# Mixture of experts: 32 slots as the stationary operand in plain float32, four column tiles of the array, weights used as they come from memory

## The chip, the cores and the metric

The kernel runs on one core of one Trainium2 chip. The metric is the device time of one launch, in microseconds (us). A core has a matrix engine (PE, with its weight loads shown apart as PEld), a vector engine (DVE), a scalar engine (ACT), a general engine (POOL) and a queue engine (SP) that here issues almost all loads; 16 DMA engines carry them out. Products are accumulated in PSUM, in banks; everything else lies in SBUF.

## The reference

Two transformer-like blocks run one after the other on 256 tokens of 1024 features, in float32. The change touches only the last stage, the mixture of experts:

```python
def expert_choice_moe(h, w_router, w_gate, w_up, w_down):
    cap = CAPACITY_FACTOR * T // N_EXPERTS                      # 2 * 256 // 16 = 32
    affinity = jax.nn.softmax((h @ w_router).astype(jnp.float32), axis=-1)
    top_vals, top_idx = lax.top_k(jnp.swapaxes(affinity, 1, 2), cap)
    xs = h[b_idx, top_idx]                                      # [16 experts, 32 slots, 1024]
    hid = jax.nn.silu(jnp.einsum('becd,edf->becf', xs, w_gate)) * jnp.einsum('becd,edf->becf', xs, w_up)
    ys = jnp.einsum('becf,efd->becd', hid, w_down) * top_vals[..., None].astype(h.dtype)
    return jnp.zeros_like(h).at[b_idx, top_idx].add(ys)
```

The block's result is `rms_norm(x + expert_choice_moe(...), norm_final_g)`. Each expert has three matrices of 1024 x 1024 float32 (4 MB each), so the stage reads 16 x 3 x 4.19 MB = 201 MB, and every weight meets only 32 token rows.

## The kernel before, in words

`body` calls `first_ffn`, `mixer`, `second_ffn`, `block2` and `moe`; what is changed lies in `moe` (L1513 on) and its helpers `raw_tile` and `expert_mm`.

Most products of this kernel are made in float32r, a rounded form of float32. So that nothing is lost, an operand is split into two float32r parts, high and low: `split` has ACT write the high part (L141, a cast) and DVE the rest (L142, a subtraction).

Weights of the experts come in raw tiles of 128 x 1024 float32 (512 KB). `raw_tile` hands out the tiles of a ring: 27 in the pool `moe_raw`, which lives from block 2 on, and 8 in `moe_raw2`, whose memory comes free when block 2 ends. SP issues one DMA for each tile (L1759), in the program's order, as soon as the tile's last user is done. Twelve turns of the ring before that serve block 2's last weights (w_proj_attn, w_out).

`expert_mm` computes one product of an expert, 32 slots by 1024 outputs, in four steps of 256 output columns. A step takes two raw tiles (4 of the 8 contraction tiles each), splits each whole tile into `whi` and `wlo` (three buffers each), and accumulates in one bank `eps` of 64 x 256: the stationary operand is 64 columns, the 32 slots' high part and their low part, and meets `whi` (L1767, L1771); the high part alone, 32 columns, meets `wlo` (L1769). The weights are the moving operand. A step's sum leaves PSUM by an ACT copy (L1777), put off into the next step.

`gate_up(e)` splits the expert's tokens into `xe` and runs the gate and up products into the two halves of `gu`. `hidden(e)` turns them on PE with the constant `stack` (L1647, which also adds the high and low rows), applies silu and the product, and splits the result into `ehid`. The down product writes `ys`, two experts in one tile; `scatter` then adds a pair of experts to the tokens' sums in four banks `acc` (L1671 puts x itself there first, L1672 the experts), with a matrix `scat` of routing weights as the stationary operand. While expert e's down product is computed, the gate and up products of e + 1 stand ahead of it in the program. After the last expert come the sums of squares (L1687), the gain (L1688), the last norm (L1722 to L1730) and the stores (L1728, L1731).

Ahead of all that, inside `moe`, the router's choice is made (L1529 to L1606) and the chosen tokens are gathered on PE into `xg` (L1577, L1616, L1617). Nothing of an expert's product can start before `xg` is there; loads into the ring can.

Of the kernel before, what the change touches and what calls it, by code (L numbers as in the profile page):

```python
# [10 lines left out]
F32 = mybir.dt.float32  # L11
# [9 lines left out]
T = 256  # L21
D = 1024
KT = 8
# [7 lines left out]
RAW, RAW2, NSPLIT, NLOW = 27, 8, 3, 3  # L31
BUFS = 1
# [9 lines left out]
LAST = 4, 2, 2  # L42
WARM = 4, 4, 0, 8, 4
FILL, FILL_RATE = 4, 0.31
HEADS = (slice(0, 64), slice(64, 128))

# [14 lines left out]
class Columns:  # L61
    """Tiles [128, n], one for every index k, to be read as [:, k, :]."""
# [8 lines left out]
class Net:  # L71
# [55 lines left out]
    def weights(self, src, ring=False):  # L127
        """src: [128, kt, columns]."""
# [57 lines left out]
    def square_sum(self, x, out, table=False):  # L186
        """out: every token's square sum over x's columns."""
# [26 lines left out]
    def row(self, a, pool, tag, blocks):  # L214
        """a, [128, 8] with a feature on every (partition, column), as a row of features on every partition, in two halves."""
# [7 lines left out]
        for n in range(2):  # L223
            # the parts of 512 features, each 128 on the partitions of their own
# [9 lines left out]
    def turned(self, ps, s, k, diag):  # L234
        """ps = 128 features of the tokens s, each times its diagonal's, the features on partitions."""
# [22 lines left out]
    def ada_pe(self, chunk, q, pool):  # L258
        """a quarter of a chunk for both streams, on TensorE: rows, then columns."""
# [16 lines left out]
    def ada_steps(self, items, pool, bufs=2):  # L276
        """items: (chunk, quarter, streams); summed over kt on VectorE and, a few steps later, over partitions on TensorE."""
# [30 lines left out]
    def ada_rows(self, pool):  # L308
        """silu of both streams' conditions as rows on every partition."""
# [5 lines left out]
    def ada_late(self, pool, rows):  # L315
        """the other chunks, from weights with the features on partitions, on VectorE: 128 features a step."""
# [27 lines left out]
    def post_row(self, pool, tag, blocks, v, g, gate, factor):  # L344
        """factor * gate * g as a row."""
# [5 lines left out]
    def postnorm(self, s, y, sums, squares, which=(0, 1)):  # L351
        """s += y / rms: y is the branch's output times post_row, sums its square sums without that; squares: s's new ones."""
# [10 lines left out]
    def products(self, s, y, out):  # L363
        """out[:, 0]: every token's square sum over y's columns; out[:, 1]: twice the sum of s * y."""
# [5 lines left out]
    def residual(self, tt, s, y, sums, sy, old):  # L370
        """As postnorm, for the tokens of tt; the new square sum and 1 / rms come from the old sum and products' sums sy."""
# [18 lines left out]
    def prenorm(self, s, v, g, shift, scale, h, squares=None):  # L390
        """h (high, low) = s / rms * g * (1 + scale) + shift for stream v, features on partitions."""
# [16 lines left out]
    def ffn_hidden(self, l, h, y, n, pl, side=iter(())):  # L408
        """The feed-forward network's products but the last: y gets the output of all but the last of FF_PARTS; returns
        that part."""  # L410
# [3 lines left out]
        for part, nt in enumerate(FF_PARTS):  # L414
# [41 lines left out]
    def out_tile(self, hid, w, tt, k0=0, k1=None, ps=None):  # L456
        """128 tokens' output, 512 columns: what the hidden tiles k0 .. k1 - 1 bring."""
# [23 lines left out]
    def first_ffn(self):  # L481
        """Both streams through the first feed-forward network; h: their normed, modulated (high, low) for the mixer."""
# [123 lines left out]
    def filter_mlp(self, pl, h3):  # L606
# [39 lines left out]
    def hyena_filter(self, pl, h3, n, dft):  # L646
        """the odd-frequency transform (real and negated imaginary part) of the filter's channels 256 n .. 256 n + 255,
        and 1 / (256 * the filter's absolute sum)."""
# [10 lines left out]
        # its high part above its low part  # L659
# [34 lines left out]
        for q, (M, x) in enumerate(((C, hp), (S, hm))):  # L694
            # the sums over the even tokens and over the odd ones give the frequencies f and 255 - f
# [16 lines left out]
    def hyena_conv(self, pl, n, dft, u, ypre):  # L712
        """ypre (per channel tile) = long_conv(u) + u * bias for the channels 512 n .. 512 n + 511."""
# [41 lines left out]
    def short_conv(self, ps, ch, out):  # L755
        """out = the depthwise convolution over three tokens of ps, channel tile ch of 24."""
# [6 lines left out]
    def rope(self, pl, ps, tab, hi, lo):  # L763
        """(hi, lo) = the rotation of ps's T columns."""
# [9 lines left out]
    def mixer_z(self, g):  # L774
        """The long convolution's input (two of the short convolution's outputs multiplied), channels 256 g .. 256 g + 255."""
# [13 lines left out]
    def mixer(self):  # L789
# [151 lines left out]
    def attend(self, pa, qq, kk, v, g, o):  # L941
        """Differential attention of the heads 2 g and 2 g + 1; o: (high, low) of the normalised output."""
# [43 lines left out]
    def plain_norm(self, s, g, h):  # L986
        """h (high, low) = s / rms * g, features on partitions."""
# [8 lines left out]
    def block2(self):  # L996
# [66 lines left out]
        for nm, shape in (("iota", [128, T + 4]), ("stack", [128, 320]), ("slotmask", [16, 128])):  # L1063
# [7 lines left out]
        with ExitStack() as es2:  # L1071
# [19 lines left out]
            def logits(c, tt):  # L1091
                """adds the features 256 c .. 256 c + 255 to the router's logits (of x not yet normed) and square sums."""
# [51 lines left out]
    def rwkv_rates(self, pr, ul):  # L1144
        """The decay rates (token-major) and the in-context learning rates of both directions, and the gate."""
# [26 lines left out]
    def rwkv_keys(self, ur):  # L1172
        """The removal direction: k * k_k, of unit length per head."""
# [15 lines left out]
    def rwkv_values(self, ur):  # L1189
        """The values token-major: [(head of the pair, token of the chunk), pair, chunk, channel]."""  # L1190
# [68 lines left out]
    def lane(self, L, p, d, ur):  # L1259
        """The recurrence of the heads 2 p (partitions 0..63) and 2 p + 1 in one direction, in 4 chunks of 64 tokens."""  # L1260
# [9 lines left out]
        # cumulated decays within the chunks, from their middle: up to and with the token, and up to the one before  # L1270
# [637 lines left out]
```

## Time and profile before

| what | value |
|---|---|
| three runs | 1908.59, 1910.38, 1912.46 us; median 1910.38 us |
| profiled execution, first to last instruction | 1910.6 us |
| busy share of the span | PE 96%, PEld 80%, DVE 78%, ACT 62%, POOL 1% |
| HBM read | 394.68 MB, 201 MB of it expert weights |
| DMA share by fortieths of the span | 9566663324321234465433311116979999999990 |
| DVE by fortieths | 5888666769978877775667777767689999999997 |

A fortieth is 47.8 us. The last two strips show where the span has a stage of another kind: from the thirtieth slice on the DMA engines and DVE are both busy 90% or more, until in the last slice the DMA engines stop and DVE does not. A busy PE says little by itself: spans of matmuls are drawn with their latency, so that short products with a wait between them still look dense.

### The profile page before, as it was taken

How to read it: one execution, taken by the hardware profiler on the slowest of the kernel's cores; microseconds unless marked ns; L12 is line 12 of the kernel's file. 1: busy time of each engine (PE TensorE's matmuls, PEld its weight loads, DVE VectorE, ACT ScalarE, POOL GpSimd, SP SyncE). 2: the span in 40 equal slices, each digit the busy share in tenths (PEclk: the TensorE clock that was granted, in tenths of full speed). 3: DMA queues.
4: the chain of work that ended last, by engine and by line, in shares of the span. 5: the costliest groups of instructions: out<-in, count | busy, mean ns of one | idle time of the engine just before them, and what ended most of it. 6: DMA issues, size and time to landing. Idle time of an engine off the chain costs nothing.

```text
span 1910.6 us, 34902 instructions
## 1 busy us (share of the span) xinstructions
PE 1828.7 (96%) x13346; PEld 1531.4 (80%) x13346; DVE 1494.8 (78%) x2966; ACT 1190.3 (62%) x2234; POOL 18.7 (1%) x36
## 2 busy tenths in 40 slices
PE   9999999999999999999999999999999999898987
PEld 5888787779988889989997888878777777676765
DVE  5888666769978877775667777767689999999997
ACT  5432223647535586564545554555589998898887
POOL 0000000000000000000000000000100000000000
PEclk9999999999999999999998999999999999999999
DMA  9566663324321234465433311116979999999990
GB/s 347 192 218 221 218 233 105 105 88 161 138 89 67 87 114 175 155 243 183 170 133 109 117 48 48 53 46 245 380 281 409 409 407 390 401 393 390 385 357 23
DMA packets 97986, 398.00 MB, mean 208 GB/s; under 512 B 12139, under 2 KB 14876, under 8 KB 83740
## 3 DMA queue, kind: packets, MB, share of 16 engines
q1 hardware_dynamic: 90720, 386.96, 54.4%
q10 hardware_dynamic: 5084, 5.14, 0.9%
q0 software_dynamic: 2016, 3.67, 0.6%
q8 instruction: 105, 1.72, 0.4%
q14 instruction: 61, 0.50, 0.1%
HBM read 394.68 MB, written 1.05 MB: 207 GB/s over the span
## 4 chain that ended last, share of the span: by engine, by line
PE 69%; DVE 13%; ACT 8%; DMA 5%; issue 4%; ACTq 0%; DVEq 0%; SPq 0%
PE mm L147 13%; PE mm L149 12%; PE mm L148 12%; DVE wlo L142 10%; ACT whi L141 5%; PE eps L1769 4%; PE at L147 4%; PE at L148 4%; PE at L149 4%; PE a L1365 3%; PE eps L1767 3%; DMA araw<-w_adat 2%; DMA raw<-exp_w_up 1%; PE at L265 1%; PE pt L1647 1%
## 5 line engine op out<-in xcount | busy, mean ns | idle before, releaser
L142 DVE TENSOR_TENSOR wlo<-raw,whi 128x512 fp32r<-128x512 f32 (+1 forms) x931 | 810.3, 906 | 118.4 <-ACT whi L141 110.5
L141 ACT CAST whi<-raw 128x512 fp32r<-128x512 f32 (+1 forms) x931 | 698.4, 795 | 266.3 <-PE mm L148 128.8
L147 PE MATMUL mm<-hh,whi 128*128 128x256 f32 (+1 forms) x800 | 253.5, 318 | 0.4 <-DVE kl L142 0.4
L149 PE MATMUL mm<-hh,wlo 128*128 128x256 f32 (+1 forms) x800 | 252.3, 318 | 0.5 <-DVE wlo L142 0.3
L148 PE MATMUL mm<-hl,whi 128*128 128x256 f32 (+1 forms) x800 | 252.3, 316 | 0.0
L1769 PE MATMUL eps<-wlo,xe 128*32 128x256 f32 x1024 | 168.3, 286 | 13.6 <-DVE wlo L142 8.4
L147 PEld LDWEIGHTS mm<-hh,whi 128*128 128x128 f32 x800 | 150.7, 189 | 15.0 <-issue 3.2
L1767 PE MATMUL eps<-whi,xe 128*64 128x256 f32 x896 | 153.2, 284 | 8.5 <-ACT whi L141 7.6
L148 PEld LDWEIGHTS mm<-hl,whi 128*128 128x128 f32 x800 | 150.7, 189 | 11.8 <-issue 1.2
L149 PEld LDWEIGHTS mm<-hh,wlo 128*128 128x128 f32 x800 | 150.3, 189 | 11.9 <-DVE wlo L142 1.3
L1769 PEld LDWEIGHTS eps<-wlo,xe 128*32 128x32 f32 x1024 | 97.0, 109 | 56.9 <-DVE wlo L142 51.1
L330 DVE SCALAR_TENSOR_TENSOR ajunk<-araw,scr 128x512 bf16<-128x512 f32 x160 | 110.3, 689 | 39.6 <-DMA araw<-w_adat 35.1
L1767 PEld LDWEIGHTS eps<-whi,xe 128*64 128x64 f32 x896 | 107.0, 135 | 22.5 <-ACT whi L141 16.7
L149 PE MATMUL at<-hh,wlo 128*128 128x512 f32 (+1 forms) x352 | 119.2, 339 | 0.0
L147 PE MATMUL at<-hh,whi 128*128 128x512 f32 (+1 forms) x352 | 119.2, 339 | 0.0
L148 PE MATMUL at<-hl,whi 128*128 128x512 f32 (+1 forms) x352 | 119.2, 339 | 0.0
L147 PE MATMUL mm<-whi,hidh 128*128 128x512 f32 x264 | 106.3, 403 | 1.8 <-ACT hidh L141 1.4
L149 PE MATMUL mm<-whi,hidl 128*128 128x512 f32 x264 | 105.1, 399 | 1.1 <-DVE hidl L142 1.1
L148 PE MATMUL mm<-wlo,hidh 128*128 128x512 f32 x264 | 105.0, 398 | 0.0
L147 PE MATMUL mm<-h2h,whi 128*128 128x256 f32 x328 | 102.0, 312 | 1.0 <-ACT gates L1048 0.8
L1769 PE MATMUL eps<-wlo,ehid 128*32 128x256 f32 x512 | 88.9, 295 | 13.9 <-DVE wlo L142 12.5
L149 PE MATMUL mm<-h2h,wlo 128*128 128x256 f32 x328 | 94.8, 290 | 1.6 <-DVE wlo L142 1.5
(605 smaller groups left out, 3629.0 us busy)
## 6 DMA issues: line engine op xcount, KB each, us to landing
raw<-exp_w_gate SPq DMA_DIRECT2D x128, 512.0 KB, 7.3
raw<-exp_w_up SPq DMA_DIRECT2D x128, 512.0 KB, 6.9
raw<-exp_w_down SPq DMA_DIRECT2D x127, 512.0 KB, 7.2
raw<-w_ff_in SPq DMA_DIRECT2D x44, 1024.0 KB, 4.9
raw<-w_in SPq DMA_DIRECT2D x32, 1024.0 KB, 4.8
araw<-w_adat SPq DMA_DIRECT2D x56, 512.0 KB, 4.4
raw<-w_ff_out SPq DMA_DIRECT2D x20, 1024.0 KB, 4.8
raw<-w_fill SPq DMA_DIRECT2D x22, 512.0 KB, 3.4
```

Of the source, the lines that this page charges most:

```text
L141: self.high = self.nc.scalar.copy(out=hi, in_=src)
L142: self.low = (eng or self.nc.vector).tensor_tensor(out=lo, in0=src, in1=hi.bitcast(F32), op=ALU.subtract)
L147: nc.tensor.matmul(out=ps, lhsT=w[0], rhs=x[0], start=first, stop=False)
L148: nc.tensor.matmul(out=ps, lhsT=w[0], rhs=x[1], start=False, stop=False)
L149: nc.tensor.matmul(out=ps, lhsT=w[1], rhs=x[0], start=False, stop=last)
L265: nc.tensor.matmul(out=ps, lhsT=self.sc[:, half * 4 + k, :], rhs=raw[:, k, :], start=(half + k == 0), stop=(half * 4 + k == 7))
L330: nc.vector.scalar_tensor_tensor(out=junk, in0=raw[:, s], scalar=1.0, in1=self.scr[v][:, s], op0=ALU.mult, op1=ALU.mult, accum_out=part[:, ...
L1365: self.nc.tensor.matmul(out=ps[r], lhsT=w[r], rhs=x[r], start=start, stop=stop)
L1647: nc.tensor.matmul(out=pt[:, f], lhsT=gu[:, f * 128:f * 128 + 128], rhs=self.stack[:, 0:2 * CAP], start=True, stop=True)
L1767: nc.tensor.matmul(out=ps, lhsT=x(k0 + k), rhs=hi[:, k, :], start=(k0 + k == 0), stop=False)
L1769: nc.tensor.matmul(out=ps[0:32], lhsT=x(k0 + k)[:, 0, :], rhs=lo[:, k, :], start=False, stop=False)
```

## The change

- The experts' weights are no longer split. A raw tile is now 128 rows of one expert matrix, all 1024 columns of them (512 KB in one piece in memory; before, 4 KB pieces at a pitch of 8 KB). Its four quarters of 256 columns are the moving operands of four plain float32 matmuls whose stationary operand is the same 128 x 32 piece of the slots; each writes its own 32 PSUM partitions (`QUARTERS`), so each uses its own 32 columns of the array. Eight raw tiles make one product, which fills one bank of 128 x 256.
- A plain float32 matmul is two matmul instructions, each with its weight load.
- `xe`, `ehid` as split pairs, the `stack` products of `hidden` and the ACT copies of the steps go. `hidden` now is two transposes and a DVE copy; silu and the product are done ahead of them on 128 x 256.
- `scatter` is called for every expert, with 32-row pieces: eight float32 matmuls of 256 columns instead of four of 512 columns for a pair.
- The tokens' sums are started (x by the identity, eight matmuls of 256 columns) ahead of the first expert.
- The ring grows from 27 + 8 to 27 + 14 raw tiles; the six come out of the split buffers' memory.
- The last expert's down product is stored once more in another order (`exp_down_last`): two raw tiles give 256 finished columns, so that the last norm's squares follow column block by column block.

```diff
-RAW, RAW2, NSPLIT, NLOW = 27, 8, 3, 3
+RAW, RAW2 = 27, 14
+QUARTERS = tuple(slice(32 * i, 32 * i + 32) for i in range(4))
...
+        acc = [self.pt(f"acc{j}", [128, 2, 256]) for j in range(4)]
+        for j in range(4):
+            for tt in range(2):
+                nc.tensor.matmul(out=acc[j][:, tt], lhsT=self.ident, rhs=x4[:, tt, j * 256:j * 256 + 256], start=(tt == 0), stop=False)
+        def load(src):
+            raw = self.raw_tile()
+            nc.sync.dma_start(out=raw, in_=src)
+            return raw
+        def product(src, x, ps, first=0):
+            for k in range(KT):
+                raw = load(src[first + k])
+                for j, q in enumerate(QUARTERS):
+                    nc.tensor.matmul(out=ps[q], lhsT=x(k), rhs=raw[:, j, :], start=(k == 0), stop=(k == KT - 1))
+                if k % 2:
+                    yield
+        def gate_up(e):
+            gates[e] = [self.pt("eps", [128, 256])]
+            x = lambda k: xg[k // 2][:, k % 2, e, :]
+            yield from product(A["exp_w_gate_2"], x, gates[e][0], e * KT)
+            gates[e].append(self.pt("eps", [128, 256]))
+            yield from product(A["exp_w_up_2"], x, gates[e][1], e * KT)
+        def activate(e):
+            g, u = gates.pop(e)
+            a = pe.tile([128, 256], F32, name="ea", tag="ea", bufs=2)
+            nc.scalar.activation(out=a, in_=g, func=AF.Silu)
...
+            nc.vector.tensor_tensor(out=a, in0=a, in1=u, op=ALU.mult)
+            return a
+        def hidden(a):
+            ps = self.pt("pt", [128, 2, 128])
+            for h in range(2):
+                nc.tensor.transpose(out=ps[:, h], in_=a[:, h * 128:h * 128 + 128], identity=self.ident)
+            hid = pe.tile([128, 2, 128], F32, name="ehid", tag="ehid", bufs=2)
+            nc.vector.tensor_copy(out=hid, in_=ps)
+            return lambda k: hid[:, k % 2, k // 2 * 32:k // 2 * 32 + 32]
+        def scatter(e, ys):
+            sc = slots(e)
             for tt in range(2):
...
+                for j, q in enumerate(QUARTERS):
+                    nc.tensor.matmul(out=acc[j][:, tt], lhsT=sc[q, tt * 128:tt * 128 + 128], rhs=ys[q], start=False, stop=False)
+        self.run(gate_up(0))
+        late = None
+        for e in range(E - 1):
+            ahead = gate_up(e + 1)
+            a = activate(e)
+            next(ahead)
+            hid = hidden(a)
+            next(ahead)
+            if late:
+                scatter(*late)
+            ps = self.pt("eps", [128, 256])
+            self.run(product(A["exp_w_down_2"], hid, ps, e * KT))
+            late = e, copy_out(ps)
+            self.run(ahead)
+        hid = hidden(activate(E - 1))
+        scatter(*late)
+        sc = slots(E - 1)
+        for j in range(4):
+            ps = self.pt("eps", [128, 256])
+            for half in range(2):
+                raw = load(A["exp_down_last"][2 * j + half])
+                for i, q in enumerate(QUARTERS):
+                    nc.tensor.matmul(out=ps[q], lhsT=hid(4 * half + i), rhs=raw[:, i, :], start=(half == 0), stop=(half == 1))
+            ys = copy_out(ps)
+            s = slice(j * 256, j * 256 + 256)
             for tt in range(2):
+                nc.tensor.matmul(out=acc[j][:, tt], lhsT=sc[:, tt * 128:tt * 128 + 128], rhs=ys, start=False, stop=(tt == 1))
             for tt in range(2):
+                nc.scalar.activation(out=sq, in_=acc[j][:, tt], func=AF.Square, accum_out=self.ss[:, tt, j:j + 1])
+                nc.vector.tensor_tensor(out=x4[:, tt, s], in0=acc[j][:, tt], in1=gfin[:, s], op=ALU.mult)
...
-    def expert_mm(self, src, e, x, out, last=False):
...
-        A[nm] = I[nm][0].reshape(16, KT, 128, 4, 256).transpose(0, 3, 2, 1, 4).reshape(64, 128, KT, 256)
+        A[nm] = I[nm][0].reshape(16 * KT, 128, 4, 256)
+    A["exp_down_last"] = A["exp_w_down_2"][15 * KT:].reshape(2, 4, 128, 4, 256).transpose(3, 0, 2, 1, 4).reshape(8, 128, 4, 256)
```

In the last expert's part the four array tiles hold four slices of the contraction, and the sum over them is made by the last `scatter` matmul, whose stationary operand has the routing matrix four times below itself. Comments and docstrings were taken out of the file too.

## Rows read from the trace of the kernel before

**Rows 1.** Windows of the span: busy us and (instructions) by engine, granted clock, DMA share, GB/s.
```profile
0.00:1325.00 1325.00, 1300.38 (x9505) 1111.88 (x9506) 975.78 (x2362) 686.26 (x1459) 11.62 (x26) 0.99 0.41 144
1325.00:1360.00 35.00, 34.06 (x280) 33.00 (x278) 26.95 (x56) 22.07 (x48) 0.00 (x0) 1.00 1.02 406
1383.00:1396.00 13.00, 11.90 (x76) 10.08 (x74) 5.69 (x13) 5.64 (x12) 0.00 (x0) 0.87 0.06 17
1396.00:1858.00 462.00, 420.99 (x3095) 331.14 (x3092) 430.43 (x446) 422.88 (x617) 0.57 (x1) 1.00 1.01 395
1858.00:1900.00 42.00, 38.07 (x271) 29.33 (x271) 38.29 (x37) 37.41 (x53) 0.00 (x0) 1.00 0.00 1
```
**Rows 2.** Groups of DVE and ACT instructions, 1400 to 1900: busy us, mean ns, idle before.
```profile
L142 DVE TENSOR_TENSOR wlo<-raw,whi 128x1024 fp32r<-128x1024 f32 x378 | 443.8, 1219 | 28.9 <-ACT whi L141 24.3 <-DMA raw<-exp_w_up 1.3
L141 ACT CAST whi<-raw 128x1024 fp32r<-128x1024 f32 x377 | 379.2, 1045 | 2.8 <-PE eps L1767 0.6
```
**Rows 3.** What the DMA queue of SP waited for, 1300 to 1911: total us, times, longest.
```profile
SPq L1759 <- DVE wlo L142: 280.1, 301, 19.6
SPq L1759 <- DMA raw<-exp_w_gate: 11.6, 13, 1.0
```
**Rows 4.** Expert loads issued at L1759, first 1320 to 1390, then 1390 to 1860.
```profile
L1759 SPq DMA_DIRECT2D raw<-exp_w_gate x16: 327/328/328, 1325.6 to 1355.9; - x16
L1759 SPq DMA_DIRECT2D raw<-exp_w_up x16: 327/328/439, 1336.6 to 1368.4; - x16
L1759 SPq DMA_DIRECT2D raw<-exp_w_down x6: 327/384/544, 1368.9 to 1373.7; - x6
L1759 SPq DMA_DIRECT2D raw<-exp_w_down x123: 327/328/582, 1394.6 to 1854.4; - x123
DMA to landing us min/median/max: 3.2/7.0/9.3
```
**Rows 5.** Timeline of PE at the experts' start: start us, us, instructions.
```profile
1389.58 0.61 PE L1624 MATMUL a<-tc,stack 64*128 64x16 f32 x4 [0.26 <-DVE tc L1621]
1390.13 1.26 PE L1671 MATMUL acc<-sx,ident 128*128 128x512 f32 x2
1390.90 1.34 PE L1767 MATMUL eps<-whi,xe 128*64 128x256 f32 x4
```
**Rows 6.** Plain float32 on PE: a run of four instructions; one line's durations; pairs of 64-column tiles.
```profile
1901.72 1.03 PE L1686 MATMUL acc<-ys,scat 128*128 128x256 f32 x4
L1509 PE MATMUL a<-krs,v x32: 378/380/431, 1249.2 to 1299.8; 128*64 128x256 f32 x32
1102.94:1103.64 0.70, 0.70 (x22) 0.70 (x22) 1.00 0.00 0
L1365 PE MATMUL a<-vtm,ak x12: 217/218/267, 1103.0 to 1103.6; 64*64 64x64 f32 x12
```
**Rows 7.** A weight load of 32 columns; transposes by the identity (groups, whole span).
```profile
L1769 PEld LDWEIGHTS eps<-wlo,xe 128*32 128x32 f32 x1024 | 97.0, 109 | 56.9 <-DVE wlo L142 51.1
L1097 PE MATMUL a<-ident,sx 128*128 128x128 f32 x16 | 3.6, 283 | 1.2 <-DVE sx L1116 1.2
```
**Rows 8.** Timeline of the end: the last copy, square, reduction, scaling and store.
```profile
1901.05 0.36 ACT L1777 COPY ys<-eps 64x256 f32<-64x256 f32 x1 [0.38 <-PE eps L1771]
1903.06 0.38 ACT L1687 ACTIVATE raw<-acc 128x256 f32<-128x256 f32 x1
1903.34 0.19 ACT L1687 ACTIVATION_READ_ACCUMULATOR raw<-acc 128x1 f32 x1
1903.91 0.15 DVE L1722 TENSOR_REDUCE fr<-ss 128x2 f32<-128x6 f32 x1
1905.13 0.82 SPq L1728 DMA_DIRECT2D out_dram<-sx  x2
```
**Rows 9.** Windows, columns as in rows 1: the granted clock about the router, and early loads.
```profile
1370.00:1373.00 3.00, 1.58 (x7) 0.62 (x6) 2.48 (x7) 2.99 (x12) 1.17 (x2) 0.58 1.01 392
15.00:20.00 5.00, 4.79 (x30) 3.33 (x31) 3.79 (x15) 2.72 (x9) 0.00 (x0) 1.00 1.03 420
```

More of the change, by code (lines that the diff above doesn't have):

```diff
@@ L1062, in block2 @@
         pc = self.pool("route_const", 1, side="right", es=self.raw_es)
[L1063 removed]
+        for nm, shape in (("iota", [128, T + 4]), ("stack", [64, 256]), ("slotmask", [16, 128])):
             t = pc.tile(shape, F32, name=nm)
@@ L1520, in moe @@
         E, CAP = 16, 32
-        col = pm.tile([128, 2, 8], F32, name="col")
-        self.sp = self.pool("moe_split", 1, es=es, side="left")
+        col = pm.tile([128, 2, E], F32, name="col")
         self.raw2 = self.pool("moe_raw2", 1, es=es, side="left")
-        self.left = None
         with ExitStack() as es2:
@@ L1623, in moe @@
             for i in range(2):
-                nc.tensor.matmul(out=ps[:, i, :], lhsT=self.stack[0:64, 64 + 128 * i:192 + 128 * i], rhs=tc, start=True, stop=True)
-            for i in range(2):
-                r = slice(64 * i, 64 * i + 64)
-                nc.vector.tensor_copy(out=col[r], in_=ps[r, :, i::2])
-        self.psum_pool("psm", eps=3, pt=1, acc00=1, acc01=1, acc10=1, acc11=1)
-        pe = self.pool("experts", 1, es=es, side="left")
-        acc = [[self.pt(f"acc{tt}{n}", [128, 512]) for n in range(2)] for tt in range(2)]
@@ L1631, in moe @@
-        gus = {}
-        yss = {}
-        def gate_up(e):
-            xe = pe.tile([128, KT, 2, CAP], F32R, name="xe", tag="xe", bufs=BUFS)
-            xq = xe.rearrange("p k q (r s) -> p k q r s", r=4)
-            for p in range(4):
-                self.split(xg[p][:, :, :, e, :], xq[:, 2 * p:2 * p + 2, 0], xq[:, 2 * p:2 * p + 2, 1])
-            gus[e] = gu = pe.tile([128, D], F32, name="gu", tag="gu")
-            for m, nm in enumerate(("exp_w_gate_2", "exp_w_up_2")):
-                yield from self.expert_mm(A[nm], e, lambda k: xe[:, k], gu[HEADS[m]])
@@ L1643, in hidden @@
-        def hidden(e):
-            gu = gus.pop(e)
-            pt = self.pt("pt", [128, KT, 2, CAP])
-            for f in range(KT):
-                nc.tensor.matmul(out=pt[:, f], lhsT=gu[:, f * 128:f * 128 + 128], rhs=self.stack[:, 0:2 * CAP], start=True, stop=True)
-            a = pe.tile([128, KT, CAP], F32, name="ea", tag="ea")
-            nc.scalar.activation(out=a, in_=pt[:, :, 0, :], func=AF.Silu)
-            if e == E - 1:
-                nc.scalar.activation(out=self.junk, in_=self.ones[:, 0:1], func=AF.Sqrt, bias=a[:, 0, 0:1])
-            nc.vector.tensor_tensor(out=a, in0=a, in1=pt[:, :, 1, :], op=ALU.mult)
-            hid = pe.tile([128, KT, 2, CAP], F32R, name="ehid", tag="ehid", bufs=BUFS)
-            self.split(a, hid[:, :, 0, :], hid[:, :, 1, :])
-            return hid
@@ L1658, in slots @@
-        def slots(g):
-            sc = pe.tile([128, T], F32, name="scat", tag="scat")
-            nc.vector.tensor_scalar(out=sc, in0=self.iota[:, 0:T], scalar1=col[:, 0, g:g + 1], scalar2=col[:, 1, g:g + 1],
+                nc.tensor.matmul(out=ps[:, i, :], lhsT=self.stack[:, 128 * i:128 * i + 128], rhs=tc, start=True, stop=True)
+            nc.vector.tensor_copy(out=col, in_=ps)
+        self.psum_pool("psm", eps=3, pt=1, acc0=1, acc1=1, acc2=1, acc3=1)
+        pe = self.pool("experts", 1, es=es, side="left")
@@ new lines, in product, with slots @@
+        def product(src, x, ps, first=0):
[5 more added lines that the diff above has]
+                    yield
+        def slots(e):
+            sc = pe.tile([128, T], F32, name="scat", tag="scat", bufs=2)
+            nc.vector.tensor_scalar(out=sc, in0=self.iota[:, 0:T], scalar1=col[:, 0, e:e + 1], scalar2=col[:, 1, e:e + 1],
@@ L1661, in slots @@
                                     op0=ALU.is_equal, op1=ALU.mult)
             return sc
-        def scatter(g):
-            sc = slots(g)
-            for tt in range(2):
-                for n in range(2):
-                    s = slice(n * 512, n * 512 + 512)
-                    if g + n == 0:
-                        nc.tensor.matmul(out=acc[tt][n], lhsT=self.ident, rhs=x4[:, tt, s], start=True, stop=False)
-                    nc.tensor.matmul(out=acc[tt][n], lhsT=sc[:, tt * 128:tt * 128 + 128], rhs=yss[g][:, s], start=(g == 0 and n == 1),
-                                     stop=(g == 6 and n == 1))
-                    if g == 6 and n == 1:
-                        nc.vector.tensor_tensor(out=x4[:, tt, s], in0=x4[:, tt, s], in1=acc[tt][n], op=ALU.add)
@@ L1677, in begin @@
-        def begin(s, *tags):
-            sums[s.start] = [self.pt(tag, [128, 256]) for tag in tags]
+        gates = {}
+        def gate_up(e):
[8 more added lines that the diff above has]
+            nc.scalar.activation(out=a, in_=g, func=AF.Silu)
+            if e == E - 1:
+                nc.scalar.activation(out=self.junk, in_=self.ones[:, 0:1], func=AF.Sqrt, bias=a[:, 0:1])
+            nc.vector.tensor_tensor(out=a, in0=a, in1=u, op=ALU.mult)
+            return a
@@ new lines, in copy_out @@
+        def copy_out(ps):
+            ys = pe.tile([128, 256], F32, name="ys", tag="ys", bufs=2)
+            nc.scalar.copy(out=ys, in_=ps)
+            return ys
+        self.run(gate_up(0))
[12 more added lines that the diff above has]
+            self.run(ahead)
@@ L1690, in moe @@
-        self.run(gate_up(0))
-        for e in range(E):
-            if e + 1 < E:
-                ahead = gate_up(e + 1)
-                next(ahead)
-            else:
-                ahead = iter(())
-                self.evacuate()
-            if e % 2 == 0:
-                if e:
-                    scatter(e // 2 - 1)
-                yss[e // 2] = pe.tile([128, D], F32, name="ys", tag="ys")
-            hid = hidden(e)
-            self.run(ahead)
-            down = self.expert_mm(A["exp_w_down_2"], e, lambda k: hid[:, k], yss[e // 2][HEADS[e % 2]], e == E - 1)
-            if e + 1 < E:
-                self.run(down)
@@ L1707, in moe @@
-        sc = slots(7)
-        gfin, sq = [self.raw_tile().rearrange("p k c -> p (k c)") for _ in range(2)]
-        nc.gpsimd.dma_start(out=gfin, in_=A["gfin"][0:1].partition_broadcast(128))
-        sums = {0: [acc[0][0], acc[1][0]]}
-        parts = slice(0, 512), slice(512, 768), slice(768, 1024)
-        begin(parts[1], "pt", "eps")
-        begin(parts[2], "acc01", "acc11")
-        for n, _ in enumerate(down):
-            if n == 3:
-                with self.tc.issue_after(self.low.ins), self.tc.issue_after(self.high.ins):
-                    finish(0, parts[0])
@@ L1878, in layout @@
     A["iota"] = np.concatenate([np.tile(np.arange(T), (128, 1)), i[:, None] + np.array([[0, 128]]), -i[:, None] - np.array([[0, 128]])], axis=1).astype(np.float32)
-    one, zero = np.eye(32), np.zeros((32, 32))
-    A["stack"] = np.block([[one, zero] + 4 * [one] + 4 * [zero], [one, zero] + 4 * [zero] + 4 * [one]]
-                          + 2 * [[zero, one] + 8 * [zero]]).astype(np.float32)
+    A["stack"] = np.kron(np.eye(2), np.tile(np.eye(32), 4)).astype(np.float32)
     return A
```

48 lines of the change are left out of this document (8 added, 40 removed).

## The prediction

> **What bounds the kernel now.** I first cut the span into windows where its character changes [rows 1]. Up to 1325 us the kernel runs code that is not changed (DMA share 0.41). From 1325 to 1360 loads for the experts fill the ring at 406 GB/s with the DMA engines full (1.02). From 1383 to 1396 the engines are almost idle (17 GB/s): the ring is full and no expert product has begun. From 1396 to 1858 the loads run at 395 GB/s on average. From 1858 to 1900 nothing is loaded any more, and DVE is still busy 38.29 of 42 us. That last window is the one to look at: 42 us of work stand behind the last load.
>
> Why it is there is told by three further views. In the groups of the experts' stretch [rows 2] one kind of DVE instruction, the low part of a raw tile's split, takes 443.8 us of 500, and what little idle time it has is a wait for its partner on ACT (24.3 us); for loads it waited 1.3 us. The queue's own waits [rows 3] say it from the other side: SP waited 301 times, 280.1 us, for that DVE instruction to give a raw tile back, and 11.6 us over loads before it. And the issues [rows 4]: 16 + 16 + 6 = 38 tiles are asked for by 1374, the next only at 1394.6, the last at 1854.4. So the ring is always full, DVE hands out one slot at a time, and the loads follow DVE's pace. Pace: (1854.4 - 1394.6) over the 346 tiles left of 384 is 1.33 us a tile; the DMA engines alone would need 0.524 MB / 406 GB/s = 1.29 us. DVE is the bound by a narrow margin, and it carries a full ring to the end.
>
> **What the change takes away.** All splits of the experts' weights: the 378 DVE and 377 ACT instructions of rows 2, and with them the end behind the last load. What is left for DVE and ACT per expert is some six instructions of 0.2 to 0.7 us, against about 31 us of loads. DVE can't stay the bound. What comes next is either the loads (24 tiles of 1.29 us, 31.0 us an expert) or PE.
>
> **What PE has to do now.** The line of 16 plain float32 matmuls with 256 moving columns and 64 stationary ones (L1509) has 32 instructions, so each is two [rows 6]. One takes 0.38 us from start to end, but four in a row end after 1.03 us, so one follows another at (1.03 - 0.38) / 3 = 0.217 us (L1686) [rows 6]. A raw tile needs four matmuls, 8 instructions: 1.73 us if they come one after another, 0.43 us if four column tiles run at once. No row before shows column tiles that share their rows. The nearest has pairs of 64 x 64 tiles with other rows and other columns: 22 instructions of 64 columns in 0.70 us, 0.032 us each, though one takes 0.217 / 4 = 0.054 us of moving columns by the figure above, so 1.7 of two ran at once [rows 6]. Bounds then are 0.43 and 1.73 us; I take 0.51 (1.7 of two scaled to 3.4 of four). The fixed rest per expert: 16 instructions of scatter, 3.5 us if one after another, and two transposes, under 0.6 us [rows 7]. So an expert costs PE 24 x 0.51 + 4.1 = 16.3 us; two tiles at a time make 24.8; one at a time 45.6. Against 31.0 us of loads the first two are hidden, the third is not. The point of change is (31.0 - 4.1) / 24 = 1.12 us a raw tile, an overlap of 1.55.
>
> The weight loads, 8 per raw tile of 0.109 us [rows 7], I cost at nothing: between 1396 and 1858 PE is busy 421.0 us and PEld 331.1 us of 462, so at least 290 us of loading lies beside matmuls, though these loads cover all 128 rows [rows 1, 7]. The Trainium skill speaks against this (TensorE: Matmul & The Clock Gate, Part 3: Packing small matmuls — row/col tiling): weight loads overlap matmuls in flight only when their row groups differ, which those of four column tiles never do. By that rule a raw tile would cost 8 x (0.109 + 0.217) = 2.6 us and the kernel about 2470 us; the rows above are against it. The same part of that page gives three column tiles a measured 2.38 times, which would make about 0.7 us a raw tile by estimate; no row here shows it.
>
> **The sum**, against the profiled span of 1910.6 us, which is the median of the runs within 0.3 us:
> - Up to the pause nothing changes. The ring of 41 takes three tiles more than the 38 of rows 4, in memory that the early splits used before. They land in the pause, which is idle [rows 1].
> - The first slot is given back when PE has done expert 0's first raw tile. xg and the stack matmuls are ready as before, at 1390.2 [rows 5]. Then stand the eight matmuls that put x into the sums: 16 x 0.217 = 3.5 us, where before two instructions and the first tile's 64-column products came. With one raw tile and the handing over about 1395; if the clock is at half there (it was at 0.58 near the router, rows 9), 1398; if the products come ahead of the sums, 1391.5. I take 1395.5, against 1394.6 before.
> - Loads left: 384 - 41 = 343 tiles and the gain row of the last norm, 344 x 0.524 MB = 180.4 MB. At 406 GB/s 444 us. The first takes 3.2 us to land [rows 4], 1.9 more than its transfer. Last landing: 1395.5 + 1.9 + 444.2 = 1841.6. PE has caught up with the ring by then: it gains 15 us on the loads in each expert, and the ring is 53 us deep.
> - Behind the last landing: 8 instructions, 0.5 + 0.17 us to drain; copy 0.36; two matmuls of float32, 1.03; two squares of 0.38 + 0.19 on ACT, one after the other; then from the reduction to the end, 1903.9 to 1910.6, 6.7 us as before [rows 8]. With 0.5 us of handing over, 10.4; 1 us more for a clock at half. I take 11.4.
>
> 1841.6 + 11.4 = **1853.0 us**, 57 less: 42 + 11 us stood behind the last load and 11.4 remain (41 us), and the loads end at 1841.6 instead of 1858 (16 us).
>
> **Rivals.**
> 1. *The array tiles don't run side by side* (the change doesn't do what it says). Place: the four matmuls of a raw tile. Price 1.73 us instead of 0.51; decides from 1.12 us up. For it: four tiles here read the same 128 rows, which no row shows; the two instructions of one matmul follow each other on the same tile, which in strict order leaves at most two at a time. Against it: the 64 x 64 pairs. 45.6 us x 16 = 730 from 1393.7, and 10.4: 2134 us, slower. The weight-load rule above (2470) is in this case's chance, at 0.01.
> 2. *Partly side by side*, between 1.12 and about 1.2 us a tile, say by weight loads that show between the tiles: PE is the bound but ahead of DVE's old pace, 1860 to 1910 us. A half clock belongs here: with loads as the bound PE pauses in every raw tile, and the granted clock fell to 0.58 where PE was busy 1.58 of 3 us [rows 9]. Four at a time at 1.2 GHz cost 0.87 us, still hidden; two at a time 1.73, but then PE has no pause left that would lower the clock.
> 3. *The loads don't get faster*, since the average of 395 GB/s has a cause of its own: only the end shrinks. 180.4 MB / 395 is 456.7 us: 1866 us. For it: the DMA share is 1.01 already [rows 1]. Against it: the same share carried 406 between 1325 and 1360, and SP was waiting for DVE.
>
> **Chances.** Forecast 0.70, with its own range 1838 to 1863: below, 420 GB/s as the early loads of larger pieces reached [rows 9] and products ahead of the sums (1391.5 + 1.9 + 429.5 + 10.4 = 1833, hardly all at once); above, 1398 and 400 GB/s. Rival 3: 0.10. Rival 2: 0.06. Rival 1: 0.14. The range 1836 to 1900 takes in the forecast, rival 3 and most of rival 2, and leaves out rival 1. Within 0.2% is about what a measurement of this kernel can tell from no change. Faster 0.84; the same 0.02, if rival 2 lands on the old pace; slower 0.14.
>
> **What would show it.** Right: no split instructions after 1390; between 1396 and the last landing 404 GB/s or more; an end of 10 to 13 us behind the last landing; PE waiting for loads; eight matmul instructions of a raw tile within 0.6 to 1.0 us; 41 tiles asked for before the pause. Wrong: raw tiles that land long before PE uses them, with the queue waiting for PE's matmuls instead of DVE, starts 0.217 us apart within a raw tile, and nothing idle on PE. An end of the loads well after 1850 with PE waiting would be rival 3.

## The result, and the profile after

The changed kernel takes 1854.38 us (1852.87 to 1856.66, 4 runs) against 1909.49 us before: ratio 0.9716, 95% interval 0.97 to 0.9731. The forecast was 1853.0. A second measurement, among the experiments, gives 0.97 (0.9686 to 0.9714). One execution stands out and is in no time below: the kernel with late sums (last experiment) once took 2614.89 us at a granted clock of 0.551, though its expert loads ran at 409 GB/s all the same.

The page after, profiled execution of 1854.9 us: engines, then the strips of DVE, granted clock and DMA over fortieths of 46.4 us.

```profile
PE 1725.6 (93%) x13314; PEld 1288.5 (69%) x13314; DVE 1040.4 (56%) x2524; ACT 741.3 (40%) x1600; POOL 18.7 (1%) x36
DVE  5789676758977877776657786867750000000001
PEclk9999999999999999999999999999999566777687
DMA  9556663323432214546542321111899999999997
```

DVE stops at the thirtieth slice, the DMA engines stay busy to the last one, and the clock strip shows something the kernel before never had: a granted clock between 0.5 and 0.9 in the last nine slices. The windows that answer to [rows 1] (busy us and instructions of PE, PEld, DVE, ACT, POOL, then clock, DMA share, GB/s):

```profile
0.00:1325.00 1325.00, 1301.24 (x9508) 1112.85 (x9509) 975.69 (x2363) 686.54 (x1459) 11.63 (x26) 0.99 0.41 144
1383.00:1396.00 13.00, 11.90 (x78) 9.25 (x80) 4.09 (x8) 2.75 (x4) 0.57 (x1) 0.87 0.34 127
1500.00:1600.00 100.00, 77.86 (x678) 23.37 (x678) 3.77 (x9) 2.27 (x6) 0.00 (x0) 0.70 1.03 409
1830.00:1840.00 10.00, 7.07 (x84) 3.28 (x80) 1.70 (x4) 1.67 (x7) 0.00 (x0) 1.00 0.85 338
1840.00:1855.00 15.00, 4.08 (x40) 2.03 (x32) 3.66 (x10) 4.92 (x17) 0.00 (x0) 0.74 0.21 79
```

Up to 1325 us nothing changed. In the experts' stretch the loads run at 409 GB/s (1500 to 1600), and the window without loads of 42 us behind the last load is gone. What the queue of SP waits for, against [rows 3], and its issues, against [rows 4] (1320 to 1390; the last group from 1390 on):

```profile
SPq L1637 <- DMA raw<-exp_w_gate: 111.9, 124, 1.8
SPq L1637 <- DMA raw<-exp_w_up: 109.7, 121, 1.8
SPq L1637 <- DMA raw<-exp_w_down: 102.7, 116, 1.1
SPq L1637 <- PE eps L1645: 29.6, 45, 16.5
```
```profile
L1637 SPq DMA_DIRECT2D raw<-exp_w_gate x17: 327/328/430, 1325.1 to 1377.3; - x17
L1637 SPq DMA_DIRECT2D raw<-exp_w_up x16: 327/328/429, 1336.4 to 1376.0; - x16
L1637 SPq DMA_DIRECT2D raw<-exp_w_down x8: 328/328/343, 1351.8 to 1360.7; - x8
L1637 SPq DMA_DIRECT2D raw<-exp_down_last x8: 328/328/328, 1822.9 to 1832.0; - x8
```

Before, 280 us of SP's waiting was for DVE to free a slot; now 324 us (the first three rows, 361 waits) is for earlier loads to land. That is how the queue looks here when the transfer itself is the bound. The wait of 16.5 us for PE is the pause before the experts. 17 + 16 + 8 = 41 tiles were asked for ahead of the pause, as forecast.

Timeline of PE, the start of the sums, the first products, and a stretch where all raw tiles lie ready (start us, us, instructions):

```profile
1389.13 5.41 PE L1630 MATMUL acc<-sx,ident 128*128 128x256 f32 x16
1394.47 3.88 PE L1645 MATMUL eps<-raw,xg 128*32 128x256 f32 x68
1399.68 2.77 PE L1645 MATMUL eps<-raw,xg 128*32 128x256 f32 x48
```

48 instructions are six raw tiles; 2.77 us less one's 0.38 makes 11 steps of 0.217 us for twelve groups of four. Four column tiles run fully side by side: 0.43 us a raw tile, the lower bound of the prediction.

### The profile page after: what moved, and what is told of

Its sections match the earlier page's. It is cut to its first block, busy times and chain, and to the rows that moved or that the text cites. A ratio compares the mean times of both kernels' runs of the same rounds, so it can differ in the third digit from the quotient of the medians.

```text
span 1854.9 us, 32911 instructions
## 1 busy us (share of the span) xinstructions
PE 1725.6 (93%) x13314; PEld 1288.5 (69%) x13314; DVE 1040.4 (56%) x2524; ACT 741.3 (40%) x1600; POOL 18.7 (1%) x36
## 4 chain that ended last, share of the span: by engine, by line
PE 70%; DMA 19%; DVE 5%; ACT 4%; issue 1%; SPq 0%; ACTq 0%; DVEq 0%
PE mm L146 14%; PE mm L148 13%; PE mm L147 13%; DMA raw<-exp_w_gate 7%; DMA raw<-exp_w_down 7%; PE at L146 4%; PE at L147 4%; PE at L148 4%; PE eps L1645 4%; PE a L1364 4%; DMA raw<-exp_w_up 3%; PE acc L1689 2%; DMA araw<-w_adat 1%; DVE wlo L141 1%; ACT whi L140 1%
## 5 line engine op out<-in xcount | busy, mean ns | idle before, releaser
L140 ACT CAST whi<-raw 128x512 fp32r<-128x512 f32 x546 | 311.3, 618 | 264.1 <-PE mm L147 129.6
L141 DVE TENSOR_TENSOR wlo<-raw,whi 128x512 fp32r<-128x512 f32 x546 | 358.5, 686 | 85.7 <-ACT whi L140 82.5
L1645 PE MATMUL eps<-raw,xg 128*32 128x256 f32 x2048 | 185.4, 489 | 30.3 <-DMA raw<-exp_w_gate 19.2
L1652 DVE TENSOR_SCALAR scat<-iota,col 128x256 f32<-128x256 f32 x16 | 6.5, 411 | 277.9 <-PE acc L1689 277.8
L148 PEld LDWEIGHTS mm<-hh,wlo 128*128 128x128 f32 x800 | 150.6, 189 | 12.1 <-DVE wlo L141 1.3
L1645 PEld LDWEIGHTS eps<-raw,xg 128*32 128x32 f32 x2048 | 61.6, 130 | 139.4 <-issue 63.1
L1645 PE MATMUL eps<-raw,ehid 128*32 128x256 f32 x960 | 101.1, 514 | 42.6 <-DMA raw<-exp_w_down 42.0
L1693 ACT COPY ys<-eps 128x256 f32<-128x256 f32 x19 | 7.0, 371 | 305.2 <-PE eps L1645 298.7
L1645 PEld LDWEIGHTS eps<-raw,ehid 128*32 128x32 f32 x960 | 23.4, 124 | 117.4 <-DMA raw<-exp_w_down 99.3
## 6 DMA issues: line engine op xcount, KB each, us to landing
raw<-exp_w_gate SPq DMA_DIRECT2D x128, 512.0 KB, 10.2
raw<-exp_w_up SPq DMA_DIRECT2D x128, 512.0 KB, 10.2
raw<-exp_w_down SPq DMA_DIRECT2D x120, 512.0 KB, 10.2
```

The lines of the kernel that those rows point to most:

```text
L140: self.high = self.nc.scalar.copy(out=hi, in_=src)
L141: self.low = (eng or self.nc.vector).tensor_tensor(out=lo, in0=src, in1=hi.bitcast(F32), op=ALU.subtract)
L1645: nc.tensor.matmul(out=ps[q], lhsT=x(k), rhs=raw[:, j, :], start=(k == 0), stop=(k == KT - 1))
L1652: nc.vector.tensor_scalar(out=sc, in0=self.iota[:, 0:T], scalar1=col[:, 0, e:e + 1], scalar2=col[:, 1, e:e + 1], op0=ALU.is_equal, op1=ALU ...
L1693: nc.scalar.copy(out=ys, in_=ps)
```

## The experiments

**Does the change need the tiles side by side?**

```diff
-  nc.tensor.matmul(out=ps[q], lhsT=x(k), ...)
+  nc.tensor.matmul(out=ps[q if k == 0 else QUARTERS[0]], lhsT=x(k), ...)      # the second run: QUARTERS[j % 2]
```

> The changed kernel, but from the second raw tile of each product on all four matmuls write the same 32 columns of the array (their sums run together, which is not the reference's product); instructions, weights and loads are as many. Theory (the four tiles must run side by side for the change to pay): a raw tile costs 8 x 0.217 = 1.73 us on PE, seven of eight of them; 16 x (14 x 1.73 + 2 x 0.43) + 15 x (7 x 1.73 + 0.43) + 15 x 3.5 = 641 us from 1394.5, then 23 us as after the last up tile: about 2060 us, PE the bound, the queue waiting for PE. Rival (PE has so much room that the order on the array does not matter): 1854 us.

> As the one before, but the four matmuls alternate between two column tiles (again sums run together). Theory (loads are the bound from 1.12 us a raw tile down): 0.86 us a raw tile, 24.4 us an expert against 31.0 us of loads: 1854 us within 3 us, with PE about twice as dense and a higher granted clock than 0.73, so also no price for the low clock. Rival (the two instructions of a matmul, or the weight loads, make two tiles slower than half of four; or the half clock comes on top): over 1.12 us a raw tile and 1870 to 2000 us.

One tile: 2025.8 us, 1.0609 of before (1.0588 to 1.063). Two tiles: 1853.54 us, 0.9709 (0.9693 to 0.9725). One column tile, PE's timeline and the queue's wait; then the windows 1396 to 1800 of one and of two tiles:

```profile
1599.80 10.52 PE L1645 MATMUL eps<-raw,xg 128*32 128x256 f32 x48
```
```profile
SPq L1637 <- PE eps L1645: 412.8, 311, 1.8
```
```profile
1396.00:1800.00 404.00, 404.00 (x2151) 206.03 (x2150) 12.19 (x29) 9.23 (x22) 0.00 (x0) 1.00 0.91 321
```
```profile
1396.00:1800.00 404.00, 367.76 (x3028) 160.85 (x3024) 18.47 (x44) 12.26 (x30) 0.00 (x0) 1.00 1.03 409
```

The same 48 instructions take 10.52 us instead of 2.77; PE never pauses, the queue waits for PE, and the change would have been a loss of 6%. So rival 1's mechanism and its price of 1.73 us a raw tile were real, only its condition was not met. Of the 34 us under the expected 2060 some 4 come from an earlier start (the products begin at 1390.8, not 1394.5). Most of the rest is scatter's: its pieces have 32 rows, and four of them run side by side too, so that an expert's 16 instructions take some 1.1 us and not the 3.5 us that I had charged. With two tiles at full clock (1.00) the time is that of four tiles at the lower one, so the low clock of the changed kernel costs nothing that the times show.

The weight loads: with one column tile every load has the rows and the columns of the matmul in flight, and one matmul follows another at (10.52 - 0.38) / 47 = 0.216 us. That alone doesn't show that the load is hidden, since 0.109 us of loading and 0.107 of streaming would add up to the same. Plain float32 matmuls of 512 columns in the kernel before settle it:

```profile
1470.15 1.02 PE L1672 MATMUL acc<-ys,scat 128*128 128x512 f32 x2
```

One of these takes 0.59 us, so the second began 0.43 us behind the first: twice as long for twice the columns, since 256 columns with an equally wide stationary operand take 0.217 [rows 6]. A part that doesn't grow with the columns, as a load in the open would be, is not there. The Trainium skill's sentence that loads overlap matmuls only across row groups (TensorE: Matmul & The Clock Gate, Part 3: Packing small matmuls — row/col tiling) doesn't hold here.

**Are the loads the bound, and how far behind is PE?**

```diff
-  raw = load(src[first + k])
+  if k % 2 == 0:
+      raw = load(src[first + k])
```

> The changed kernel with every second raw tile of the products not loaded: the one before is used twice (the products are then not the reference's). 196 expert tiles instead of 384. Theory (loads are the bound, PE at full clock needs 14 to 16 us an expert): loads end at 1395.2 + 1.9 + 156 x 1.28 = 1597, PE's own work is then the bound, 376 x 0.43 + 15 x 3.5 + stalls: 1640 to 1690 us, clock near 1. Rival (PE at the low clock is close behind the loads, 0.86 us a raw tile and no faster): 1394 + 376 x 0.86 + 52 + 23: about 1800 us. Rival (something else than loads bounds the changed kernel): over 1820.

1617.26 us, 0.847 of before (0.8453 to 0.8487): under the range that I gave. The loads still ran at full rate; a window, and scatter in PE's timeline:

```profile
1396.00:1580.00 184.00, 182.23 (x3018) 100.28 (x3010) 18.47 (x44) 10.87 (x29) 0.00 (x0) 1.00 1.03 406
```
```profile
1507.64 1.15 PE L1690 MATMUL acc<-ys,scat 32*128 32x256 f32 x16
```

With a load for every second raw tile the DMA engines are as full as before (406 GB/s), and the last load lands at 1598, where the theory had 1597. But 18 us stand behind it, against 12.7 in the changed kernel, so PE was a little late there: the two are close to even. An expert has 12 loads of 1.28 us, 15.4 us. PE, at full clock and nearly without a pause, takes 12.1 us for one at 1500 (24 x 0.43 and about 1.6 for scatter and transposes) and 16.8 at 1570, where scatter stands in pieces between the raw tiles. Against the 31 us of loads in the changed kernel that leaves PE about half of its time free, or more.

**Was DVE the bound before, and not PE?**

```diff
-  self.split(raw, hi[:, 0:kt], lo[:, 0:kt])
+  m = kt // 2
+  self.split(raw[:, 0:m], hi[:, 0:m], lo[:, 0:m])
...
-  nc.tensor.matmul(out=ps, lhsT=x(k0 + k), rhs=hi[:, k, :], ...)
+  nc.tensor.matmul(out=ps, lhsT=x(k0 + k), rhs=hi[:, k % m, :], ...)          # lo alike
```

> The kernel before with only the first half of each raw tile split (DVE and ACT instructions of half the columns) and used twice by the matmuls: PE's work and the loads are as before, half of the weights have no part in the products. Theory (the splits on DVE bounded the kernel before, PE did not): DVE falls to some 0.69 us a raw tile, the loads are the bound at 1.29 us, the ring drains before the end, so nothing stands behind the last load but the last tile's work: 1394.6 + 1.9 + 347 x 1.29 + 11: about 1855 us. Rival (PE, busy 91% of the stretch in the profile, was the bound): 1900 to 1910 us.

1861.26 us, 0.9747 (0.9728 to 0.9767). In the experts' stretch, first the window, then DVE's group, then the queue's wait:

```profile
1396.00:1800.00 404.00, 388.72 (x3013) 325.42 (x3011) 250.02 (x435) 273.74 (x599) 0.57 (x1) 1.00 1.03 406
```
```profile
L142 DVE TENSOR_TENSOR wlo<-raw,whi 128x512 fp32r<-128x512 f32 x372 | 249.1, 690 | 135.2 <-ACT whi L141 129.0 <-PE eps L1770 2.0 <-PE eps L1772 0.8
```
```profile
SPq L1759 <- DMA raw<-exp_w_up: 112.0, 125, 1.8
```

All of PE's float32r products stayed, and 49 of the 55 us came; the time is 6 us over the expected 1855. PE's "busy 91%" in the kernel before was no bound; the splits on DVE and ACT were. This run halves both, so it doesn't tell the two apart: that DVE's part came last rests on [rows 2] and [rows 3]. Half the splits would have been enough to come to the loads' pace, 406 GB/s with the old order of the weights in memory. So the new order can be worth no more than the step from 406 to 409, some 3 us.

**What is the ring's depth worth?** Six raw tiles fewer, in the changed kernel (`RAW2 = 8`) and in the kernel before (`RAW2 = 2`).

> The changed kernel with the ring of before, 27 + 8 raw tiles instead of 27 + 14. Theory (loads are the bound, and the pause before the experts is the only place where they stand still): six tiles fewer land in the pause, 6 x 1.28 = 7.7 us later at the end: 1862 us, +0.4%. Rival (the ring is deep enough at 35; depth only covers jitter): 1854 us, no difference.

> The kernel before with a ring of 27 + 2 raw tiles instead of 27 + 8. Theory (DVE was the bound, so raw tiles that lie ready gain nothing): the loads end some 8 us later, the work behind the last load shrinks by as much, the time is that of before within 2 us. Rival (the loads bounded it, at 395 GB/s): +7.7 us, 1917 us.

Changed kernel: 1863.76 us, 0.976 of before (0.9746 to 0.9774), so 8 to 11 us over the changed kernel's own 0.97 and 0.9716, which were measured apart from it. Its trace gives the size better: from the first load after the pause to the last it took 444.5 us (1396.4 to 1840.9), and in the changed kernel 436.8 (1395.2 to 1832.0), 7.7 us less, as expected. Before: 1909.86 us, 1.0003 (0.9994 to 1.0012). The same six tiles are worth nothing where the splits set the pace and their full transfer time where the loads do. The kernel before with the short ring shows the trade in its windows: its loads end later, in a window in which nothing was loaded before [rows 1], and the end stays where it was.

```profile
1858.00:1866.00 8.00, 7.27 (x55) 5.87 (x54) 8.00 (x9) 6.24 (x8) 0.00 (x0) 1.00 0.65 237
1866.00:1900.00 34.00, 30.85 (x223) 24.46 (x222) 29.96 (x30) 30.64 (x49) 0.00 (x0) 1.00 0.00 1
```

**The two ends of the loads.** First the eight matmuls that start the sums move behind `self.run(gate_up(0))`; then, on top of it, the end of the last expert is put in another order.

> The changed kernel with the eight matmuls that put x into the sums moved behind expert 0's gate and up products. Theory (the pause of the loads is time lost in full): they take 5.4 us on PE ahead of the first product (1389.1 to 1394.5, at half clock for 3.4 us), the loads go on 4.5 to 5 us earlier and end as much earlier: -4.5 to -5 us, 1849.5 us, -0.25%. Rival (the DMA engines catch up, or the end hangs on something else): within 1 us of 1854.

> As the one before, and in the last expert's four column blocks the next block's products stand ahead of this block's addition to the sums, and the copy out of PSUM is made by DVE instead of ACT. Theory (in the changed kernel the last block's copy waits 1.2 us behind squares on ACT and its products 0.4 us behind the addition): another -1 to -2 us on the one before, 1848 us. Rival (the last load's landing alone sets the end): the same as the one before.

0.9703 of before for both (0.9689 to 0.9717; 0.969 to 0.9716): too close to the changed kernel's 0.9716, which was measured apart from them, to show the 4.5 to 5 us of the first theory or the 1 to 2 us of the second. So all were measured once more side by side, with a third variant:

```diff
+            if j:
+                add(j - 1, ys)                # the two matmuls into the sums, behind block j's products
             ys = copy_out(ps)                 # on ACT, ahead of the squares of block j - 1
+            if j:
+                squares(j - 1)
+                gain(j - 1)                   # one product for both token tiles
...
         nc.vector.tensor_reduce(out=r, in_=self.ss, axis=AX.X, op=ALU.add)
+        gain(3)
```

> The changed kernel once more, beside the next three on the same chip: 1854 us, 0.971 to 0.972 of before.

> The sums started behind expert 0's gate and up products, as in the run above of that name. Theory (the pause of the loads counts in full): 4.5 to 5 us under the changed kernel of this call. Rival: within 1 us of it.

> With the end reordered as in the run above of that name, where DVE's copies stand behind its two gain products of the block before. Theory (that copy and the additions behind it wait as long as the copies on ACT did): within 1 us of the one before it in this call. Rival (the products standing ahead save 1 to 2 us).

> The sums late; at the end the next block's products ahead of the addition, the copy out of PSUM on ACT ahead of the squares of the block before, one gain product for both token tiles, and the last reduction ahead of the last gain product. Theory (behind the last landing stand only its matmuls, copy, addition, two squares and the norm): copy 1.2 us earlier, one gain of 0.7 us beside the square root instead of 0.86 ahead of it: 1.5 to 2.5 us under the late sums alone, 6 to 7 under the changed kernel. Rival (the last load's landing moves as little as the measurement tells): no difference from the late sums.

| kernel | us, median of 5 | of before | 95% interval |
|---|---|---|---|
| changed | 1852.37 | 0.97 | 0.9686 to 0.9714 |
| sums late | 1850.11 | 0.9688 | 0.9672 to 0.9704 |
| sums late, copies on DVE | 1853.68 | 0.971 | 0.9695 to 0.9724 |
| sums late, copy before squares | 1848.62 | 0.9676 | 0.9662 to 0.969 |

Only one pair is told apart by these times: the last variant from the one with copies on DVE (0.969 against 0.9695). The interval of the last meets that of the changed kernel by 0.0004, and the late sums are not told from anything. The traces, one execution of each, show what the edits did. Two timelines, of the changed kernel and then with late sums (the last write of the gathered tokens, the sums, the first products, the first loads after the pause), and behind them the issues of the last loads of each, in the same order:

```profile
1384.42 0.75 DVE L1615 TENSOR_SCALAR xg<-a,pv 128x512 f32<-128x512 f32 x1 [1.11 <-PE a L1574]
1386.16 3.72 PE L1630 MATMUL acc<-sx,ident 128*128 128x256 f32 x16
1389.81 6.47 PE L1645 MATMUL eps<-raw,xg 128*32 128x256 f32 x116
1390.51 1.28 SPq L1637 DMA_DIRECT2D raw<-exp_w_gate  x3
```
```profile
1386.64 0.75 DVE L1615 TENSOR_SCALAR xg<-a,pv 128x512 f32<-128x512 f32 x1 [1.11 <-PE a L1574]
1388.37 7.11 PE L1642 MATMUL eps<-raw,xg 128*32 128x256 f32 x128
1389.07 1.28 SPq L1634 DMA_DIRECT2D raw<-exp_w_gate  x3
```
```profile
L1637 SPq DMA_DIRECT2D raw<-exp_down_last x8: 327/327/355, 1818.1 to 1827.1; - x8
```
```profile
L1634 SPq DMA_DIRECT2D raw<-exp_down_last x8: 327/328/328, 1817.8 to 1826.8; - x8
```

The gathered tokens are ready at 1385.2 in the one and 1387.4 in the other (1388.2 in the first profile of the changed kernel): the unchanged code ahead varies by 3 us, as much as the edits are worth. From there the loads go on after 5.3 us in the changed kernel and 1.7 us with late sums, 3.6 us earlier. From first to last issue they then take 436.6 against 437.7 us, so 1.1 us of it is given back; why was not settled. The net by these two executions is 2.5 us, about half of what I expected; the medians differ by 2.3, which the intervals don't tell from nothing. My 4.5 to 5 us had counted 5.4 us for the sums, which was their price at the low clock; at full clock they take 3.7.

At the end, from the last landing (10.1 us behind the last issue) to the last instruction: changed 1837.2 to 1849.9, 12.7 us; sums late 12.7; copies on DVE 13.6; copy before squares 1840.0 to 1851.1, 11.1 us. Its last two blocks:

```profile
1838.87 1.13 PE L1716 MATMUL acc<-ys,scat 128*128 128x256 f32 x4 [0.49 <-ACT ys L1690]
1839.93 1.07 PE L1731 MATMUL eps<-raw,ehid 128*32 128x256 f32 x16
1840.61 0.38 ACT L1720 ACTIVATE sq<-acc 128x256 f32<-128x256 f32 x1
1841.07 0.37 ACT L1690 COPY ys<-eps 128x256 f32<-128x256 f32 x1
1841.50 1.13 PE L1716 MATMUL acc<-ys,scat 128*128 128x256 f32 x4 [0.49 <-ACT ys L1690]
1843.74 0.16 DVE L1741 TENSOR_REDUCE fr<-ss 128x2 f32<-128x8 f32 x1 [1.93 <-ACT sq L1720]
1843.81 0.68 DVE L1724 TENSOR_TENSOR sx<-acc,gfin 128x512 f32<-128x512 f32 x1
```

So by the traces this variant saves 1.6 us at the end, within the 1.5 to 2.5 expected, and putting the copies on DVE loses 0.9 (there they stand behind the two gain products). It does not save it in the way that its diff says. The engines did not run the blocks in the order of the source: block 2's addition (1838.87) still stands ahead of block 3's products (1839.93), and the squares of block 2 (1840.61) ahead of the last copy (1841.07), as in the changed kernel. What the trace shows changed is that one gain product in place of two no longer stands between the two squares, so that they end sooner and the copy starts 0.07 us behind its products instead of 0.44; and that the reduction runs ahead of the last gain product (1843.74, 1843.81). How much of the 1.6 us each brings was not separated, and products ahead of the additions were not tried.

Two expectations were missed. The copies on DVE were to stay within 1 us of the late sums, and their median is 3.6 us higher. The last variant was to come out 6 to 7 us under the changed kernel, and it is 3.75 under; its median is the lowest of all kernels run.

## Why the prediction was right, step by step

- *DVE bounds the kernel before, by a narrow margin.* Shown for the splits: halving them on DVE and ACT alone gives 0.9747, and six ring tiles less cost nothing. That it was DVE's half rests on the waits of the trace before.
- *Column tiles overlap.* The step rested on pairs with other rows and columns. Measured 0.43 us, at the lower bound (0.51 taken); one column tile for seven raw tiles of eight loses 6%. This is the one step that could have turned the sign, and the trace of before didn't hold the evidence: a good guess, from the nearest rows.
- *Weight loads cost nothing.* Shown with one column tile and the 512-column matmuls. The prediction's own ground, PE and PEld busy at the same time, was weak: PE's busy time is drawn with its latency.
- *Loads go on at 1395.5.* 1395.2 in the first profile, but 1390.5 in the second: right in mechanism (the sums stand ahead), with a spread of 3 us from the code ahead that I had not allowed for and some 2 us from the clock. That the first profile agrees to 0.3 us is luck: the sums began 1.1 us earlier than assumed (1389.1) and took 1.9 us longer (5.4).
- *Loads at 406 GB/s, last landing 1841.6.* 409 GB/s; last issue 1832.0 and 10.1 us to landing: 1842.2. Here too two misses cancel. At 409 GB/s the 180.4 MB take 441.0 us and not 444.2, but 447.0 passed, so that 6.0 us come on top and not 1.9: I had sized that from the shortest landing before (3.2 us), and with the queue full a load takes 10.2 us.
- *11.4 us behind the last landing.* 12.7. The size was off because the place was: I had the last block wait for its loads alone. In fact the four blocks run in a rhythm of their own behind the last up tile, 2.95 us each: products, copy, addition, and only then the next block's products. The last block's products began 0.6 us behind the last landing, and its copy 0.44 us behind the products, since the squares of the block before were still on ACT:

```profile
1842.73 1.07 PE L1719 MATMUL eps<-raw,ehid 128*32 128x256 f32 x16
1843.87 0.38 ACT L1725 ACTIVATE sq<-acc 128x256 f32<-128x256 f32 x1 [0.49 <-DVE sx L1726]
1844.24 0.36 ACT L1693 COPY ys<-eps 128x256 f32<-128x256 f32 x1
1844.65 1.13 PE L1723 MATMUL acc<-ys,scat 128*128 128x256 f32 x4 [0.85 <-ACT ys L1693]
1847.70 0.15 DVE L1728 TENSOR_REDUCE fr<-ss 128x2 f32<-128x8 f32 x1
```
- *PE 16.3 us an expert.* At full clock 12.1 us was measured, and 16.8 where scatter stands in pieces. Scatter was charged 3.5 us and takes 1.15 in one piece, a raw tile 0.51 and takes 0.43. All of it is hidden behind the loads, so the time didn't feel it.

## What to carry to other kernels

When a ring of loads is full from its first round to its last, look to the engine that frees the slots for the bound, however full the DMA engines look; the work that stands behind the last load is what a faster consumer wins first. A count of instructions on PE says little where small tiles can lie side by side: ask first whether they overlap, and find the overlap at which the bound changes sides. Once the loads are the bound, what stands ahead of the first freed slot counts, down to matmuls that merely stand early in the program: six ring tiles cost their full 7.7 us here, and of 3.6 us won ahead of the slot 2.5 were left at the last load. And read the order of the engines from the trace, not from the source: an edit that moves lines need not move instructions.

## What was not expected of the hardware

TensorE's granted clock moved between its two levels (1.2 and 2.4 GHz) all through the experts' stretch, 0.70 on average from 1500 to 1600; between most raw tiles there PE paused, waiting for the next load. One raw tile at either level (granted 0.50 and 1.00):

```profile
1501.16 1.08 PE L1645 MATMUL eps<-raw,ehid 128*32 128x256 f32 x8 [0.20 <-DMA raw<-exp_w_down]
1524.40 0.64 PE L1645 MATMUL eps<-raw,xg 128*32 128x256 f32 x8 [0.31 <-DMA raw<-exp_w_gate]
```

Both are under the 1.28 us of a load. With the same products on two column tiles, where PE paused less (busy 367.76 of 404 us), it was 1.00 throughout. And the DMA engines don't end together: in the profile of the changed kernel the rate falls in the last windows of 2 us, though all eight last loads had been issued by 1832.

```profile
1834.00:1836.00 2.00, 1.30 (x17) 0.62 (x18) 0.15 (x1) 0.37 (x1) 0.00 (x0) 1.00 0.98 393
1836.00:1838.00 2.00, 1.90 (x20) 0.86 (x19) 0.42 (x1) 0.57 (x3) 0.00 (x0) 1.00 0.63 254
1840.00:1842.00 2.00, 1.15 (x18) 0.56 (x11) 0.85 (x2) 1.13 (x5) 0.00 (x0) 1.00 0.17 68
```
